# Side steps of layer 0's attention laid over a whole head, with one PSUM bank for V's sums and one for small uses

## The chip, the cores and the metric

One core of one Trainium2 chip. The metric is the device time of one execution in microseconds (us); lower is better. A core has a matrix engine (TensorE, PE in the profile; loading its weights is shown as PEld) and four others: VectorE (DVE), ScalarE (ACT), GpSimd (POOL) and SyncE (SP), which issues most transfers. Each engine carries out its own instructions in order, and waits at the first that is not ready. Data lie in SBUF (128 partitions) and matrix products are summed in PSUM, eight banks of 128 x 512 f32.

## The reference, cut to what matters

Two layers of a diffusion backbone over 1024 latent tokens and 256 context tokens, each with 1024 features. Layer 0, the one that is changed, is a multi-head latent attention with 16 heads: queries and keys have 64 columns of their own and 32 columns that are turned by a rotary table (the key's 32 are shared by all heads), values have 64.

```python
def project(t, rope):
    q_lat, kv_lat, k_pe, gate = split(t @ w_in)
    q  = (rms_norm(q_lat, g_qa) @ w_qb).reshape(b, n, 16, 64 + 32)
    kv = (rms_norm(kv_lat, g_kva) @ w_kvb).reshape(b, n, 16, 64 + 64)
    q_nope, q_pe = q[..., :64], q[..., 64:]
    k_nope, v    = kv[..., :64], kv[..., 64:]
    if rope:                      # latent tokens only
        q_pe, k_pe = apply_rope(q_pe, cos, sin), apply_rope(k_pe, cos, sin)
    return concat(q_nope, q_pe), concat(k_nope, k_pe for all heads), v, gate

o   = softmax(q   @ concat(k, k_c).T * scale) @ concat(v, v_c)   # 1024 latent queries, 1280 keys
o_c = softmax(q_c @ k_c.T * scale) @ v_c                         # 256 context queries, 256 keys
```

Layer 1 is a differential attention over the same tokens; it is not changed.

## The kernel before

Numbers are kept as pairs of f16 (a high part and the rest, H and L in the names), and a product is three matmuls: high by high, high by low, low by high. The attention of layer 0 runs from 250 to 772 us of the span, head after head (`for h in range(H0)`, the loop at the end of what is printed below). Tokens stand in three chunks of queries: b=0 and b=1 of 512 latent tokens, b=2 of 256 context tokens.

**A unit** (`units0`) is two key tiles of 128 for one chunk. `st_of` makes the scores, six matmuls of 512 columns (L834 to 836) into a pair of banks from `pair()`; ACT takes the exponential (L778) and rounds it to f16, `ph` (L779); POOL makes the rest, `pl` (L780). Two units later (`LAG`) `retire` multiplies with V: 24 matmuls (L846, L848, L849), in two halves of 12, summing over the chunk's units in one bank d. Column 64 of V is one, so the bank also holds the row's sum. Behind the last unit of a chunk `fin` divides on DVE: a reciprocal (L857) and a multiply (L858), and bank d is free after it. A head has five units for b=0, five for b=1 and one, of half the size, for b=2.

**Side steps** stand between the units on PE and make what a later chunk or head needs. `max0` finds each query's largest score: for b=0 and b=1 four wide pieces (two matmuls L758 into a pair, a reduction on DVE L760), a piece over the context keys (L764, L765, L766), then a transpose of the result on PE (L769), which DVE writes into rows of Q (L770); `st_of` of that chunk reads them. `prod_k` and `prod_q` make a head's keys and queries: `proj_pair` multiplies for two heads at once (L186 to 188), wide for 1024 latent tokens and small for 256 context tokens; `split16` makes the high part on ACT (L182) and the low part on DVE (L183); transfers on SP (`dmv`) bring the rows to the tiles KH, KL and q. Once in four heads the queries' rotary columns are made too, tile stp; their latent part goes through `rope` on DVE: a shuffle (L291), a multiply from PSUM (L292), two operations with both inputs in SBUF (L295, L296). `load_outw` (heads 13 to 15) prepares the output weights on ACT and DVE, `h1_range` (head 2) makes a scale for layer 1 in a chain of small DVE operations.

**What sets the order.** PE's order is the order of the code (`manual_schedule` with `MAN = 'P'`). The order on ACT, DVE, POOL and SP is set by a scheduler when the kernel is built, and is fixed then. `run_step` walks a list of units: the unit's `st_of`; the first half of the side steps due at it; the first half of `retire`; the other side steps; the second half of `retire`. Which steps are due is told by generators with a count for each unit. A head is two such walks, b=0, and b=1 with b=2. `set_banks(a=3, d=2)` gives three pairs to everything but V's sums, and two banks d to these.

Head numbers in this text count from 0. "Even" and "odd" heads are those numbers; keys and queries of heads 2m and 2m+1 are projected together.

Of the kernel before, what the change touches and what calls it, by code (L numbers as in the profile page):

```python
# [17 lines left out]
P = 128  # L18
# [3 lines left out]
CTX = 256  # L22
# [8 lines left out]
DQ = NOPE + ROPE  # L31
# [23 lines left out]
def hybrid_kernel(  # L55
# [690 lines left out]

    def max0(h, b):
# [14 lines left out]
        ps = pair()[:, :nt * CTX].rearrange("p (a b) -> p a b", a=nt)  # L762
# [5 lines left out]
        bk = pair()  # L768
# [116 lines left out]
    set_banks(a=3, d=2)  # L885
# [20 lines left out]
    yctx = {}  # L906
    for h in range(H0):
        last = h == H0 - 1
        even, quad = (h + 1) % 2 == 0, (h + 1) % 4 == 0
        if h == H0 - 2:  # L910
            rp.close()
            ow = ow_ctx.enter_context(spool("o0w", side="right"))
            oH = ow.tile([P, KT, D], F32R, name="oH0")
            oL = ow.tile([P, KT, D], F32R, name="oL0")
            lw = load_outw(oH, oL, lambda: w0("ows"))
        if last:
            run_step(units0(h, 0) + units0(h, 2), [(max0(h, 2), (1, 0, 1)), (max0(h, 1), (0, 1, 1, 1, 2, 1)),
                                                   (lw, (1, 0, 1))])
            octx = {t: (w0(b_), w0(a_))[::-1] for t, a_, b_ in ((8, "rsw", "rr"), (9, "cs", "cs"))}

            def load_ctx():
                yield
                yield
# [4 lines left out]
                yield  # L928

            run_step(units0(h, 1), [(load_ctx(), (1, 1, 1))])  # L930
            tv = lambda x: x.bitcast(F32R).rearrange("p (a b) -> p a b", a=KT)
            tctx = {8: (tv(w0("ows")), tv(w0("ows"))), 9: (tv(w0("rr")), tv(w0("cs")))}
            with tc.manual_schedule(engines={ENG[c] for c in MAN}):
# [7 lines left out]
                for t in (8, 9):  # L941
                    y_ = pair()
                    yctx[t] = [y_[:, :512], y_[:, 512:] if t == 8 else bank("d")]
                    for hh in range(2):
# [4 lines left out]
                        flush()  # L949
        else:  # L950
            kq = chain(prod_k(h + 1), prod_q(h + 1, 0))
            low = [[(first(lw, 3), p_)] if h == H0 - 2 else [] for p_ in ((1, 0, 1, 0, 1), (1, 0, 1, 0, 1))]
            if h == 2:
                ab1_of()
            hr = [(h1_range(pair), (0, 1, 0, 1, 1))] if h == 2 else []
            run_step(units0(h, 0), hr + [(max0(h, 1), (1, 1, 2, 1, 1)), (max0(h, 2), (0, 1, 0, 1)),
                                    (kq, (2, 2, 1 + quad, 0, 0) if even else (2,))] + low[0])
            qs = chain(prod_q(h + 1, 1), prod_q(h + 1, 2))
            run_step(units0(h, 1) + units0(h, 2), [(max0(h + 1, 0), (1, 1, 1, 2, 1)),
                                                   (qs, (1, 1 + quad, 0, 1) if even else (2,))] + low[1])  # L960
# [757 lines left out]
```

## Time and profile before

| what | value |
|---|---|
| time, median of 3 runs | 1767.51 us (1767.5 to 1769.69) |
| span of the profiled execution | 1767.7 us, 36788 instructions |
| TensorE busy (whole span) | 1660.4 us, 94% |
| VectorE, ScalarE, GpSimd busy | 1224.6 (69%), 1118.5 (63%), 821.9 us (46%) |
| layer 0's attention, 16 heads | 250.4 to 772.2 us, 521.8 us |

The page shows one execution; its span stands 0.2 us over the median. A busy engine is not one at its peak: a TensorE instruction is shown with its latency, and consecutive matmuls overlap, so the time that a matmul takes from the next is the difference between their starts. PEclk is the clock that the engine was granted, as a share of its full rate of 2.4 GHz; 0.50 is the lower level, 1.2 GHz. In a timeline the square bracket behind an operation holds how long its engine stood idle just before it and the operation that ended this.

### The profile page before, as it was taken

What the parts mean: (1) busy time and instruction counts of PE and PEld (TensorE: products, weight loads), DVE (VectorE), ACT (ScalarE), POOL (GpSimd) and SP (SyncE); (2) the same over time, 40 slices, a digit from 0 to 9 for tenths busy, and PEclk for the clock granted to TensorE, in tenths of its full rate; (3) what the DMA queues carried; (4) which work ended last, traced back from release to release, by engine and by line L of the source; (5) the groups of instructions that cost most, each with busy time, mean ns of one, the idle gap of its engine ahead of it and who ended that gap; (6) DMA issues with size and microseconds to landing.
All of it is one profiled execution on the core that took longest, in us unless ns stands there. A gap on an engine that the chain in (4) does not pass through costs nothing. (4 is left out here: it accounts for less than half of the span.)

```text
span 1767.7 us, 36788 instructions
## 1 busy us (share of the span) xinstructions
PE 1660.4 (94%) x14564; PEld 1231.8 (70%) x14564; DVE 1224.6 (69%) x2037; ACT 1118.5 (63%) x2235; POOL 821.9 (46%) x740
## 2 busy tenths in 40 slices
PE   7999989999999998899999999999999999987998
PEld 6999956556666655577867676767676767666876
DVE  7658666565565666646856778787878787878664
ACT  3551177777777778845635676767676767758542
POOL 1432147667767776845552323241424233354454
PEclk9999999999999999999999999999999999999999
DMA  8258520110111122245522222231212222142331
GB/s 308 81 152 259 166 68 21 43 44 22 42 46 25 39 57 62 65 168 196 167 96 64 80 68 80 67 81 55 60 51 63 60 58 75 32 125 66 112 108 72
DMA packets 111225, 154.84 MB, mean 88 GB/s; under 512 B 13415, under 2 KB 84679, under 8 KB 111054
## 3 DMA queue, kind: packets, MB, share of 16 engines
q1 hardware_dynamic: 102654, 144.90, 27.3%
q10 hardware_dynamic: 8400, 7.61, 1.3%
q8 instruction: 114, 1.87, 0.4%
q14 instruction: 57, 0.47, 0.1%
HBM read 98.65 MB, written 27.07 MB: 71 GB/s over the span
## 5 line engine op out<-in xcount | busy, mean ns | idle before, releaser
L780 POOL TENSOR_TENSOR pl<-p,ph 128x1024 f16<-128x1024 f32 (+1 forms) x176 | 364.3, 2076 | 148.4 <-ACT ph L779 122.6
L1371 ACT ACTIVATE p<-ps_b,mx 128x512 f32<-128x512 f32 (+1 forms) x384 | 230.2, 617 | 58.9 <-DVE mx L1367 57.4
L778 ACT ACTIVATE p<-ps_a,esc 128x1024 f32<-128x1024 f32 (+1 forms) x176 | 189.0, 1074 | 94.8 <-PE ps_a L836 88.8
L760 DVE TENSOR_REDUCE mx<-ps_a 128x1 f32<-128x1024 f32 x128 | 155.3, 1222 | 129.9 <-PE ps_a L758 129.8
L779 ACT CAST ph<-p 128x1024 f16<-128x1024 f32 (+1 forms) x176 | 177.1, 1006 | 5.5
L1365 DVE TENSOR_REDUCE mx<-ps_b 128x1 f32<-128x512 f32 x256 | 164.9, 680 | 0.7 <-PE ps_b L1349 0.7
L849 PE MATMUL ps_d<-Vh,pl 128*128 128x65 f16 x1344 | 146.0, 194 | 4.4 <-POOL pl L780 4.4
L846 PE MATMUL ps_d<-Vh,ph 128*128 128x65 f16 x1344 | 148.2, 195 | 0.0
L848 PE MATMUL ps_d<-Vl,ph 128*128 128x64 f16 x1344 | 147.0, 193 | 0.0
L846 PEld LDWEIGHTS <-ph 128*128 128x128 f16 x1344 | 123.3, 97 | 18.1 <-issue 4.9
L848 PEld LDWEIGHTS <-ph 128*128 128x128 f16 x1344 | 124.0, 98 | 12.2 <-issue 0.3
L1348 PE MATMUL ps_b<-KS,QS 128*128 128x512 f16 (+1 forms) x384 | 126.5, 347 | 5.9 <-DVE pl L183 2.9
L1349 PE MATMUL ps_b<-KS,Q 128*128 128x512 f16 (+1 forms) x384 | 129.7, 347 | 0.0
L834 PE MATMUL ps_a<-qH,KH 100*128 100x512 f16 x320 | 121.9, 381 | 7.8 <-ACT p L778 3.5
L1396 POOL TENSOR_TENSOR sm<-sm,us 128x1 f32<-128x1 f32 x64 | 18.5, 289 | 234.3 <-DVE sm L1375 221.2
L849 PEld LDWEIGHTS <-pl 128*128 128x128 f16 x1344 | 123.2, 97 | 5.8 <-POOL pl L780 5.8
L1384 PE MATMUL ps_b<-idr,p 128*128 128x128 f32 x640 | 103.8, 278 | 24.2 <-ACT p L1371 6.2
L183 DVE SCALAR_TENSOR_TENSOR pl<-ps_b,lcf,ph 128x512 f16<-128x512 f32 (+1 forms) x192 | 116.9, 653 | 11.2 <-ACT ph L182 11.2
L182 ACT ACTIVATE ph<-ps_b,lcf 128x512 f16<-128x512 f32 (+1 forms) x192 | 115.2, 647 | 13.9 <-PE ps_b L1384 13.8
L835 PE MATMUL ps_a<-qH,KL 96*128 96x512 f16 x320 | 121.8, 381 | 0.0
L836 PE MATMUL ps_a<-qL,KH 96*128 96x512 f16 x320 | 121.2, 379 | 0.0
L1384 PEld LDWEIGHTS ps_b<-idr,p 128*128 128x128 f32 x640 | 78.2, 143 | 49.0 <-ACT p L1371 11.6
(438 smaller groups left out, 5290.7 us busy)
## 6 DMA issues: line engine op xcount, KB each, us to landing
ws<-in_dw SPq DMA_DIRECT2D x28, 512.0 KB, 3.9
adw<-in_ada_w SPq DMA_DIRECT2D x24, 512.0 KB, 4.6
adaw<-in_ada_w SPq DMA_DIRECT2D x16, 512.0 KB, 7.3
g<-sg_d SPq DMA_DIRECT2D x16, 512.0 KB, 8.5
sg_d<-gg ACTq DMA_DIRECT2D x40, 128.0 KB, 3.6
o_d<-op SPq DMA_DIRECT2D x7, 640.0 KB, 3.8
xt<-in_xT SPq DMA_DIRECT2D x16, 256.0 KB, 4.4
wgs<-in_w_in SPq DMA_DIRECT2D x32, 128.0 KB, 3.1
```

The lines of the kernel that those rows point to most:

```text
L760: dve.tensor_reduce(mx[:, t, 0:1], ps, axis=AX.X, op=ALU.max)
L778: act.activation(p32[:, :n], st, AF.Exp, scale=esc0)
L779: act.copy(ph[:, :n], p32[:, :n])
L780: pool.tensor_tensor(pl[:, :n], p32[:, :n], ph[:, :n], op=ALU.subtract)
L846: pe.matmul(pv[:, t, :], ph[:, ts], Vh[:, k, h, :], start=(k == kcs[0] and t == 0), stop=False, skip_group_check=True)
L848: pe.matmul(pv[:, t, :V0], ph[:, ts], Vl[:, k, h, :], start=False, stop=False, skip_group_check=True)
L849: pe.matmul(pv[:, t, :], pl[:, ts], Vh[:, k, h, :], start=False, stop=(k == NT - 1), skip_group_check=True)
L1348: pe.matmul(out, qs[m][:, ts], ks[m][:, c0:c0 + n], start=True, stop=False)
L1349: pe.matmul(out, q1[m][:, ts], ks[m][:, c0:c0 + n], start=False, stop=True)
L1365: dve.tensor_reduce(mx[:, 2 + 2 * m + i:3 + 2 * m + i], b, axis=AX.X, op=ALU.max, negate=True)
L1371: act.activation(p[m][:, c0:c0 + n], b, AF.Exp, bias=nb, accum_out=sm[:, 2 + 3 * m + i:3 + 3 * m + i])
L1384: pe.transpose(st[:, j * P:(j + 1) * P], pc[:, (k0 + j) * P:(k0 + j + 1) * P], idn)
```

## The change

It rewrites the stage's plan and its use of PSUM; each engine has as many instructions as before.

- `set_banks(a=3, d=1, e=1)`: V's sums have one bank instead of two, and a bank e is new. `small()` hands it out, in place of a pair, to the context projections, to the context piece of b=2's row maximum, to all transposes of `max0` and to `h1_range`.
- `run_step` takes a dictionary. `sides[k, i]` lists the steps at unit k, ahead of the first (i=0) or second (i=1) half of `retire`. A head is one walk of 11 units.
- `part_k`, `part_q`, `part_p`, `load_k`, `load_q` and `top_of` take the place of the generators. In even heads the wide query projection for the pair of heads that follows now stands at unit 9, and, once in four heads (2, 6, 10), the wide rotary projection with its rope at unit 10: both stood in the odd head before. In odd heads the wide key projection stays in unit 0, the small projections in units 1 and 2.

```diff
+    def small():
+        return bank("e") if "e" in banks else pair()
     def proj_pair(cw, w2, src2, c0, n):
-        ps = pair()
+        ps = small() if n == CTX else pair()
...
+    def part_p(h, b):
+        if b == 0:
+            stH["p"] = stage("stp")
+        sH, sL = stH["p"]
+        c0, n = TOK[b]
+        cw = 1024 + (h // 4) * P
+        src = proj_pair(slice(cw, cw + P), WQ2, QS2, c0, n)
+        if b == 0:
+            sw, r = w0("rsw"), w0("rr")
+            for _ in rope(src, n, cosA, sinA, sw, r):
+                pass
+            src = r[:, :n]
+        split16(sH[:, c0:c0 + n], sL[:, c0:c0 + n], src, qsc0)
...
-        ps = pair()[:, :nt * CTX].rearrange("p (a b) -> p a b", a=nt)
+        ps = (pair if b < 2 else small)()[:, :nt * CTX].rearrange("p (a b) -> p a b", a=nt)
...
-        bk = pair()
+        bk = small()
         pe.matmul(bk[:nt, :P], ng[:, :nt], idr, start=True, stop=True)
...
+                for i in range(2):
+                    for f, *a in sides.get((k, i), ()):
+                        f(*a)
+                    if old:
+                        retire(i)
...
-    set_banks(a=3, d=2)
+    set_banks(a=3, d=1, e=1)
...
+        if h == 0:
+            put(0, 0, top_of, h, 1)
+        for k, i in ((0, 0), (1, 0), (2, 0), (3, 0), (4, 0)):
+            put(k, i, top_of, h, 1)
+        put(5, 1, top_of, h, 2)
+        put(6, 1, top_of, h, 2)
+        if n % 2:
+            put(0, 0, load_k, n)
+            put(0, 0, load_q, n, 0)
+            if n + 1 < H0:
+                put(9, 0, part_q, n + 1, 0)
+                if (n + 1) % 4 == 0:
+                    put(10, 1, part_p, n + 1, 0)
         else:
+            put(0, 1, part_k, n, 0)
+            put(1, 0, part_k, n, 1)
+            put(1, 1, part_q, n, 1)
+            put(1, 1, load_k, n)
+            put(1, 1, load_q, n, 0)
+            if n % 4 == 0:
+                put(2, 1, part_p, n, 1)
+        for k in (4, 5, 6, 7, 8):
+            put(k, 0, top_of, n, 0)
+        put(9, 1, top_of, n, 0)
+        put(6, 0, load_q, n, 1)
+        put(7, 0, load_q, n, 2)
+        put(10, 0, top_of, n, 1)
+        if h == H0 - 2:
+            for k in (0, 2, 4, 5, 7, 9):
+                put(k, 0, next, lw, None)
+        if h == 2:
+            ab1_of()
+            hr = h1_range(lambda: bank("e"))
+            for k in (1, 3, 4):
+                put(k, 0, next, hr, None)
+        run_step(units0(h, 0) + units0(h, 1) + units0(h, 2), at)
```

`n` is the next head, h + 1. In the rows below a name ends in the number of its tile; `mx` is a row maximum, `rc` and `op` are the reciprocal and the result of `fin`, `stk`, `stq` and `stp` the split keys, queries and rotary columns, `ps_a` a pair, `ps_d` and `ps_e` the single banks.

VectorE in the first units of head 3, which carries the rotary projection of the heads behind it. Before:

```order
L760 TENSOR_REDUCE mx_4315<-ps_a_4317 128x1
L857 RECIPROCAL rc_4362<-ps_d_4149 128x4
L183 SCALAR_TENSOR_TENSOR stkL_4322<-ps_a_4323,ksc_69,stkH_4321 128x1024
L183 SCALAR_TENSOR_TENSOR stkL_4322<-ps_a_4344,ksc_69,stkH_4321 128x256
L858 TENSOR_TENSOR op_4128<-ps_d_4149,rc_4362 128x4x64
L760 TENSOR_REDUCE mx_4315<-ps_a_4378 128x1
```

After, at the same place (the shuffle reads the pair that the projection at the end of head 2 filled):

```order
L291 STREAM_SHUFFLE rsw_4316<-ps_a_4303 128x1024
L292 TENSOR_TENSOR rr_4317<-ps_a_4303,cs_2545 128x1024
L295 TENSOR_TENSOR rsw_4316<-rsw_4316,cs_2549 128x1024
L813 TENSOR_REDUCE mx_4283<-ps_a_4352 128x1
L296 TENSOR_TENSOR rr_4317<-rr_4317,rsw_4316 128x1024
L183 SCALAR_TENSOR_TENSOR stkL_4369<-ps_a_4370,ksc_69,stkH_4368 128x1024
L903 RECIPROCAL rc_4391<-ps_d_4144 128x4
L813 TENSOR_REDUCE mx_4283<-ps_a_4407 128x1
L183 SCALAR_TENSOR_TENSOR stpL_4302<-rr_4317,qsc_70,stpH_4301 128x1024
L904 TENSOR_TENSOR op_4117<-ps_d_4144,rc_4391 128x4x64
L183 SCALAR_TENSOR_TENSOR stkL_4369<-ps_e_4411,ksc_69,stkH_4368 128x256
```

The rope, with its split stpL, now stands ahead of the multiply L904 that ends chunk b=1 of head 2.

VectorE at the start of head 5, an odd head without a rotary projection. Before:

```order
L760 TENSOR_REDUCE mx_5390<-ps_a_5392 128x1
L857 RECIPROCAL rc_5437<-ps_d_5224 128x4
L183 SCALAR_TENSOR_TENSOR stkL_5397<-ps_a_5398,ksc_69,stkH_5396 128x1024
L183 SCALAR_TENSOR_TENSOR stkL_5397<-ps_a_5419,ksc_69,stkH_5396 128x256
L858 TENSOR_TENSOR op_5203<-ps_d_5224,rc_5437 128x4x64
L760 TENSOR_REDUCE mx_5390<-ps_a_5453 128x1
L765 TENSOR_REDUCE mx_5457<-ps_a_5459 128x2
```

After:

```order
L903 RECIPROCAL rc_5437<-ps_d_5213 128x4
L904 TENSOR_TENSOR op_5186<-ps_d_5213,rc_5437 128x4x64
L183 SCALAR_TENSOR_TENSOR stkL_5415<-ps_a_5416,ksc_69,stkH_5414 128x1024
L813 TENSOR_REDUCE mx_5352<-ps_a_5453 128x1
L183 SCALAR_TENSOR_TENSOR stkL_5415<-ps_e_5457,ksc_69,stkH_5414 128x256
L903 RECIPROCAL rc_5493<-ps_d_5463 128x2
L183 SCALAR_TENSOR_TENSOR stqL_5296<-ps_e_5470,qsc_70,stqH_5295 128x256
```

Here the multiply stands ahead of the wide key split, and the small key split (from bank e) behind it and a row maximum; the small query projection takes bank e next.

## Rows read from the trace of the kernel before

**Rows 1.** Page, part 1: busy time, share of the span, instructions of each engine.

```profile
PE 1660.4 (94%) x14564; PEld 1231.8 (70%) x14564; DVE 1224.6 (69%) x2037; ACT 1118.5 (63%) x2235; POOL 821.9 (46%) x740
```

**Rows 2.** Windows, heads 2 to 5 and 13; columns PE, PEld, DVE, ACT, POOL, PEclk, DMA.

```profile
311.60:344.19 32.59, 29.03 (x358) 18.00 (x355) 19.84 (x38) 22.78 (x23) 22.38 (x12) 0.95 0.16 43
344.19:383.29 39.10, 36.23 (x399) 23.96 (x396) 26.42 (x34) 27.28 (x29) 23.26 (x12) 1.00 0.11 26
383.29:410.97 27.68, 26.84 (x353) 16.82 (x350) 16.37 (x23) 22.78 (x23) 22.40 (x12) 1.00 0.20 52
410.97:444.79 33.82, 32.42 (x381) 21.02 (x377) 20.01 (x27) 25.69 (x27) 22.46 (x12) 1.00 0.12 28
...
667.81:704.51 36.70, 32.92 (x381) 21.07 (x377) 25.65 (x31) 29.34 (x30) 23.26 (x11) 1.00 0.21 56
```

**Rows 3.** Timeline of PE, one unit of head 4: start, length, operation, tiles, count.

```profile
399.26 0.38 PE L834 MATMUL ps_a<-qH,KH 100*128 100x512 f16 x1
...
400.56 0.59 PE L758 MATMUL ps_a<-KH,qH 96*128 96x512 f16 x2
400.99 0.20 PE L846 MATMUL ps_d<-Vh,ph 128*128 128x65 f16 x1
...
401.71 0.38 PE L834 MATMUL ps_a<-qH,KH 100*128 100x512 f16 x1
```

**Rows 4.** Timeline of PE, head 5: wide and small query projection, and what follows each.

```profile
417.99 0.50 PE L186 MATMUL ps_a<-latH,wqH 128*128 128x512 f32 x1
...
420.85 0.20 PE L846 MATMUL ps_d<-Vh,ph 128*128 128x65 f16 x1
...
434.34 0.36 PE L186 MATMUL ps_a<-latH,wqH 128*128 128x256 f32 x1
...
435.14 0.20 PE L846 MATMUL ps_d<-Vh,ph 128*128 128x65 f16 x1
```

**Rows 5.** Timeline of ACT, POOL and DVE in the unit of rows 3.

```profile
400.82 1.11 ACT L778 ACTIVATE p<-ps_a,esc 128x1024 f32<-128x1024 f32 x1 [0.26 <-PE ps_a L836]
403.14 2.13 POOL L780 TENSOR_TENSOR pl<-p,ph 128x1024 f16<-128x1024 f32 x1 [0.32 <-ACT ph L779]
401.19 1.23 DVE L760 TENSOR_REDUCE mx<-ps_a 128x1 f32<-128x1024 f32 x1 [1.23 <-PE ps_a L758]
402.54 0.42 DVE L858 TENSOR_TENSOR op<-ps_d,rc 128x256 f32<-128x256 f32 x1
```

**Rows 6.** Groups by line and shape, 270 to 765 us: count, busy, mean ns, idle.

```profile
L183 DVE SCALAR_TENSOR_TENSOR stkL<-ps_a,ksc,stkH 128x1024 f16<-128x1024 f32 x7 | 9.0, 1284 | 0.9
L183 DVE SCALAR_TENSOR_TENSOR stkL<-ps_a,ksc,stkH 128x256 f16<-128x256 f32 x7 | 3.3, 475 | 0.0
```

**Rows 7.** Timeline of DVE and POOL around the rope in head 3.

```profile
354.28 1.29 DVE L291 STREAM_SHUFFLE rsw<-ps_a 128x1024 f32<-128x1024 f32 x1
357.85 1.23 DVE L296 TENSOR_TENSOR rr<-rr,rsw 128x1024 f32<-128x1024 f32 x1
360.32 1.84 DVE L183 SCALAR_TENSOR_TENSOR stpL<-rr,qsc,stpH 128x1024 f16<-128x1024 f32 x1
358.15 2.93 POOL L780 TENSOR_TENSOR pl<-p,ph 128x1024 f16<-128x1024 f32 x1 [3.64 <-ACT ph L779]
```

**Rows 8.** Timeline of PE: waits in head 2, and two waits in layer 1.

```profile
326.35 0.22 PE L769 MATMUL ps_a<-idr,ng 128*4 128x128 f32 x1 [1.50 <-DVE hm L301]
328.33 0.49 PE L834 MATMUL ps_a<-qH,KH 100*128 100x512 f16 x1 [1.38 <-DVE qH L770]
997.92 0.33 PE L1384 MATMUL ps_b<-idr,p 128*128 128x128 f32 x1 [2.34 <-ACT rr L1314]
1616.76 0.48 PE L1384 MATMUL ps_b<-idr,p 128*128 128x128 f32 x1 [5.57 <-DVE pl L183]
```

**Rows 9.** Windows, two stretches at the lower clock; columns as in rows 2.

```profile
328.46:331.87 3.41, 3.41 (x13) 1.33 (x12) 0.04 (x1) 0.83 (x1) 0.57 (x1) 0.50 0.00 0
1615.30:1622.10 6.80, 5.34 (x19) 2.57 (x20) 5.35 (x9) 6.37 (x18) 5.03 (x2) 0.50 0.86 302
```

More of the change, by code (lines that the diff above doesn't have):

```diff
@@ L745, in prod_q, with part_k, part_q, load_k @@
         yield
+    def part_k(h, b):
+        if b == 0:
+            stH["k"] = stage("stk")
+        sH, sL = stH["k"]
+        c0, n = TOK[b]
+        split16(sH[:, c0:c0 + n], sL[:, c0:c0 + n], proj_pair(slice(h * NOPE, h * NOPE + P), WK2, KS2, c0, n), ksc0)
+    def part_q(h, b):
+        if b == 0:
+            stH["q"] = stage("stq")
+        sH, sL = stH["q"]
+        c0, n = TOK[b]
+        split16(sH[:, c0:c0 + n], sL[:, c0:c0 + n], proj_pair(slice(h * NOPE, h * NOPE + P), WQ2, QS2, c0, n), qsc0)
+    def part_p(h, b):
+        if b == 0:
+            stH["p"] = stage("stp")
+        sH, sL = stH["p"]
+        c0, n = TOK[b]
+        cw = 1024 + (h // 4) * P
+        src = proj_pair(slice(cw, cw + P), WQ2, QS2, c0, n)
+        if b == 0:
+            sw, r = w0("rsw"), w0("rr")
[3 more added lines that the diff above has]
+        split16(sH[:, c0:c0 + n], sL[:, c0:c0 + n], src, qsc0)
+    def load_k(h):
+        i = h % 2
+        r = slice(i * NOPE, i * NOPE + NOPE)
+        for K_, j in ((KH, 0), (KL, 1)):
+            dmv(K_[i][:NOPE, :], stH["k"][j][r, :])
+    def load_q(h, b):
+        c0, n = CHUNKS[b]
+        tg = "q" if n == 512 else "qc"
+        qt[h, b] = w0(tg + "H"), w0(tg + "L")
+        r = slice((h % 2) * NOPE, (h % 2) * NOPE + NOPE)
+        rr = slice((h % 4) * ROPE, (h % 4) * ROPE + ROPE)
+        for j in range(2):
+            dmv(qt[h, b][j][:NOPE, :], stH["q"][j][r, c0:c0 + n])
+            dmv(qt[h, b][j][NOPE:DQ, :], stH["p"][j][rr, c0:c0 + n])
     def max0(h, b):
@@ L906, in hybrid_kernel, with top_of @@
     yctx = {}
+    tops = {}
+    def top_of(h, b):
+        if (h, b) not in tops:
+            tops[h, b] = max0(h, b)
+        next(tops[h, b], None)
     for h in range(H0):
         last = h == H0 - 1
-        even, quad = (h + 1) % 2 == 0, (h + 1) % 4 == 0
+        n = h + 1
         if h == H0 - 2:
@@ L915, in hybrid_kernel, with put @@
             lw = load_outw(oH, oL, lambda: w0("ows"))
+        at = {}
+        def put(k, i, *what):
+            at.setdefault((k, i), []).append(what)
         if last:
[L917 to L918 removed]
+            put(0, 0, top_of, h, 2)
+            put(2, 0, top_of, h, 2)
+            for k, i in ((0, 1), (1, 0), (2, 1), (3, 0), (4, 1)):
+                put(k, i, top_of, h, 1)
+            for k in (0, 2):
+                put(k, 1, next, lw, None)
+            run_step(units0(h, 0) + units0(h, 2), at)
             octx = {t: (w0(b_), w0(a_))[::-1] for t, a_, b_ in ((8, "rsw", "rr"), (9, "cs", "cs"))}
             def load_ctx():
[L922 to L923 removed]
                 for t in (8, 9):
@@ L942, in hybrid_kernel @@
                     y_ = pair()
-                    yctx[t] = [y_[:, :512], y_[:, 512:] if t == 8 else bank("d")]
+                    yctx[t] = [y_[:, :512], y_[:, 512:] if t == 8 else bank("e")]
                     for hh in range(2):
@@ L949, in hybrid_kernel @@
                         flush()
-        else:
[L951 to L960, printed above, removed]
+            continue
+        if h == 0:
+            put(0, 0, top_of, h, 1)
+        for k, i in ((0, 0), (1, 0), (2, 0), (3, 0), (4, 0)):
+            put(k, i, top_of, h, 1)
+        put(5, 1, top_of, h, 2)
[7 more added lines that the diff above has]
+                    put(10, 1, part_p, n + 1, 0)
+        else:
+            put(0, 1, part_k, n, 0)
[20 more added lines that the diff above has]
+        run_step(units0(h, 0) + units0(h, 1) + units0(h, 2), at)
     a0.close()
```

15 lines of the change are left out of this document (1 added, 14 removed).

## Prediction

> **What bounds the kernel now.** The list of engines comes first: TensorE is busy for 94% of the span, the next engine for 70% [rows 1]. So the end is set by TensorE's work and by the moments at which it stands. The windows by head come second, since they show where it stands. A head's fixed work can be counted from one unit: scores take 1.30 us (399.26 to 400.56), a wide piece of the row maximum 0.43, the sums with V 0.72, and the unit 2.45 in all [rows 3]. A head has ten such units, but eight wide pieces: 10 x (1.30 + 0.72) + 8 x 0.43 = 23.6. The context unit, half as large, adds 1.0; the ten matmuls of the context pieces, half as wide as those of a wide piece (0.215 each), 1.1; three transposes some 0.2. That is 26.0 us. Head 4, which has no projection of its own, took 27.68 [rows 2]: it stands for 1.7. Head 5 carries a wide query projection of 2.86 (417.99 to 420.85) and a small one of 0.80 [rows 4], and the keys' with half as many matmuls (1.43 and 0.40): 31.5 of work in 33.82, so 2.3 of standing. Head 3 has a wide and a small rotary projection besides (2.86 and 0.8): 35.1 of work in 39.10, 4.0 of standing. The pair 4/5 thus stands for 4.0, the pair of a plain even head and head 3 for 5.7. Over the whole stage that is some 50 us. The last view is the timeline of the other engines in one unit: exponential, rounding and POOL's operation (1.11, 1.2 with the gaps from 401.93 to 403.14, and 2.13, [rows 5]) follow each other at a rhythm of 2.45, and DVE has a maximum of 1.23 and little else; so between side steps nothing but TensorE is full, and every stall comes from a step that puts several DVE or ACT operations at one place.
>
> **What the change removes and adds.** The work of every engine stays as it is; only standing and clock can change.
>
> *Ordinary pairs* (0/1, 4/5, 8/9, 12/13). The wide query projection goes to unit 9 of the even head, one wide maximum stands in nearly every unit, and the small uses no longer take pairs from the scores. The scores' waits for a pair, most of the 4.0, should go. About 0.4 stays in the first unit of a head, where the context unit before it is short and POOL's pl comes late, and 0.1 for bank d. New is a wait at bank e: in units 0 and 1 of an odd head the small key and the small query projection take the one bank e with only six matmuls of V (0.2) between. From the head's start TensorE reaches the second at 1.30 + 0.43 + 0.36 + 1.43 + 0.36 + 1.30 + 0.43 + 0.40 + 0.2 = 6.2. DVE must first read bank e for the small key split, which its order puts behind the wide one and a maximum. The wide high part on ACT ends at 4.9 (scores 1.6 from 399.26 to 400.82, exponential 1.1, rounding 1.1, and the split, which I take as long as the exponential of the same shape, 1.1); then come the wide low part, 1.28, the maximum at a spacing of some 1.13, and the small split, 0.475 [rows 5, 6]: 7.8. The wait is 1.65. Queued behind it on TensorE are the rest of V's sums and the next scores, so it is on the path. Sum: 0.5 + 1.65 + 0.15 = 2.3 against 4.0, **a gain of 1.7** for each of four pairs, 6.8. The wait's bounds are 0.9 (the maximum overlapping more) and 2.2.
>
> *Heads 14 and 15.* The output weights' steps cost head 13 some 2.9 us (36.70 against 33.82, [rows 2]) and are spread as before, so I leave their cost as it is. Head 14 loses the ordinary standing and the break between its two walks, head 15 some of the first. I take **2.0** for both, between 0 and 3.
>
> *Pairs with a rotary projection* (2/3, 6/7, 10/11). Here the place decides. The wide rotary projection now ends in the last unit of the even head, and its whole chain on DVE stands ahead of the multiply that frees bank d, of which there is only one. TensorE needs that bank for the context unit's first sum, in unit 1 of the odd head. Its work from the end of the projection to there is 0.36 + 1.30 + 0.43 + 0.36 + 1.43 + 0.36 + 1.30 + 0.43 + 0.40 = 6.4. DVE's is: shuffle to last rope operation 3.45 (354.28 to 357.85, less a reciprocal of 0.12, [rows 7]), a maximum 1.13, the last rope operation 1.2, the wide key split 1.2, the reciprocal 0.15, a maximum 1.13, stpL 1.28, the multiply 0.42 [rows 5], and 0.4 for starts between engines: 10.4. The stall is 4.0 if no operation is held up. But the last rope operation and stpL read two tiles of SBUF, and rows show what such an operation and POOL's do to each other. POOL's op at 358.15 took 2.93 instead of 2.13, its first 0.9 us being those until the rope operation of 357.85 ended; stpL, begun at 360.32, took 1.84 and ended 1.08 after POOL was done at 361.08 [rows 7]. Whichever starts first, the other waits for its end. Counted from the projection's end, POOL starts unit 0's operation at 0.36 + 3.9 = 4.2 (3.9 from scores to POOL, 399.26 to 403.14), and the rope operation is ready at 4.7 to 4.8, so it waits 2.13 - 0.55 = 1.6. stpL is ready at 10.0; POOL's next start comes at 9.9, since ACT has to make stpH between the exponential and the rounding of unit 1; so stpL waits between nothing and 2. I take 0.4 for it, near the 0.56 by which stpL was longer in rows 7. The stall is then **6.0**, bounds 4.0 and 7.6. The standing of the pair becomes 6.0 + 0.5 + 0.8 (first unit and small waits at bank e, most of which passes while TensorE stands) = 7.3 against 5.7: **a loss of 1.6**.
>
> The Trainium skill (SBUF — State Buffer, "Who interferes with whom") says the same of a VectorE instruction with two SBUF inputs and a GpSimd instruction that reads SBUF, and that reductions never contend. By that rule the two maxima in the chain cost nothing more, as in the sum, and stpL would wait either nothing or for a whole operation, never 0.4: 5.6 or 7.6 in place of 6.0. The rows so far agree with it.
>
> *The clock.* Rows show what happens to the granted clock behind such a stall. In head 2, after waits of 1.50 and 1.38 close together, it was at 0.50 (1.2 GHz) for 3.41 us, all of it busy; after a wait of 5.57 it was at 0.50 for 6.80, of which TensorE was busy for 5.34; after a wait of 2.34 there was no fall [rows 8, 9]. A stall of 6.0 is nearest to that of 5.57. Work at half rate costs half its time, so a fall costs between 1.7 (3.41 / 2) and 2.7 (5.34 / 2): I take **2.2** for each of the three pairs. The Trainium skill ("TensorE: Matmul & The Clock Gate", Terms) takes the whole time at the lower clock for its penalty, not the busy part; by that it would be 3.4 each and the sum 3.6 later, which no row bears out.
>
> *Heads 2 and 3* have h1_range as well. Before, its chain of small DVE operations made waits of 1.50 and 1.38 [rows 8]. Now it stands ahead of the write of b=1's row maxima into Q, and scores wait there; the chain is the same, so I take nearly the same, 2.7, between 1.4 (one of the two) and 3.2. Before: 32.59 + 39.10 = 71.7 with 61.1 of work, so 10.6, of which 1.5 to 1.7 was clock. After: 7.3 + 2.7 = 10.0 and 2.2 of clock. **A loss of 1.6** in all; if the clock falls a second time there, 1.7 more.
>
> **Sum.** Gains 6.8 + 2.0 = 8.8. Losses 2 x (1.6 + 2.2) + 1.6 = 9.2. The profiled execution took 1767.7, the median is 0.2 lower; 1767.7 + 0.4 - 0.2 gives **1768**. What this kernel's measurement can tell from no change is about 0.2%, 3.5 us: faster means below 1764.0, slower above 1771.0. So the forecast is no change, out of two halves that cancel.
>
> **Rivals.**
> *B, the rotary chain is cheaper than I have it.* If the clock does not fall behind the three stalls, 6.6 us come back: 1761.5. The wait of 2.34 without a fall speaks for it; the stall's length, two and a half times that, against. If the operations also miss POOL's and the stall is 4.0, 6.0 more: 1755.5. It decides from two of the three falls missing. Chance 0.29, most of it near 1761.5.
> *C, slower: the clock falls behind the bank e waits too.* Each of heads 1, 5, 9 and 13 has the wait of 1.65, close behind the first unit's 0.4; in head 2 two waits of 1.4 to 1.5 were enough for a fall. Four falls at 1.7 give 6.8: 1775. It decides from two of them on. Against it stands the 2.34 without a fall. With it goes, at 1772, the rotary stall at its upper bounds (7.6, and 2.7 of clock). Chance 0.33.
> *D, the change does not do what it says.* The idle for pairs is merely renamed: scores wait for the same readers as before, and ordinary pairs gain 0 instead of 1.7, while the rotary pairs escape both losses because DVE is reached earlier. The even heads, whose standing of 1.7 has no projection in it, speak for it a little. 1767.7 less about 1: also no change. Chance 0.06.
>
> **How the numbers follow.** Forecast 0.32 and D 0.06 give 0.38 within 0.2%; B 0.29 faster; C 0.33 slower. The range takes in B's likelier value and C: 1759 to 1777. Left out are B's lower end and C with both its parts.
>
> **What would show it.** Right: in heads 3, 7 and 11 TensorE waits 5 to 7 us at the context unit's first product with V, released by DVE's multiply, and the granted clock is 0.50 right behind it; in heads 5 and 9 the small query projection waits some 1.6 for DVE's small stkL; heads 4 and 5 take 59.8 together, 6 and 7 about 70.6. Wrong: clock at 1.00 behind the rotary stall (B), at 0.50 in heads 5 and 9 (C), the multiply ahead of stpL in time, or scores that still wait for a pair in units 2 to 8 (D). The prediction falls as a whole if the stall at bank d is below 3 us, since then nothing cancels the gains.

## The result, and the profile after

The changed kernel takes 1775.04 us (median), the kernel before 1767.51: a ratio of 1.0039, 95% interval 1.0024 to 1.0053 (the two medians alone give 1.0043, inside it). It is slower, by more than the 0.2% that the measurement can tell from no change. The prediction said 1768, no change, between 1759 and 1777: the time lies inside, the likeliest case was not the one that came. The profiled execution has a span of 1773.6 against 1767.7.

The stage's heads first, from the windows of the kernel after (start and end, length, busy time and count of PE, PEld, DVE, ACT, POOL, then PEclk, DMA share, GB/s). Shown are heads 2 to 7, 11 and 13, and the three stretches at the lower clock in heads 3, 7 and 11:

```profile
313.83:348.19 34.36, 32.61 (x382) 21.54 (x378) 21.63 (x42) 24.60 (x25) 25.30 (x13) 1.00 0.16 44
348.19:387.31 39.12, 32.37 (x375) 21.03 (x371) 27.69 (x32) 25.50 (x26) 19.55 (x10) 0.91 0.10 23
387.31:416.25 28.94, 28.94 (x366) 18.75 (x363) 17.12 (x25) 24.15 (x25) 24.13 (x12) 1.00 0.19 50
416.25:447.06 30.81, 29.23 (x369) 18.94 (x366) 19.81 (x28) 24.42 (x25) 20.73 (x11) 1.00 0.13 30
447.06:479.08 32.02, 31.98 (x377) 20.99 (x374) 18.47 (x27) 24.59 (x25) 25.30 (x13) 1.00 0.18 47
479.08:517.63 38.55, 31.81 (x374) 20.90 (x371) 27.68 (x32) 25.49 (x26) 19.54 (x10) 0.91 0.10 24
609.52:649.36 39.84, 33.09 (x374) 21.28 (x371) 27.69 (x32) 25.49 (x26) 19.55 (x10) 0.87 0.13 36
678.31:715.39 37.08, 31.65 (x368) 19.68 (x365) 29.20 (x36) 31.27 (x33) 21.62 (x10) 0.95 0.40 113
358.75:365.57 6.82, 4.45 (x24) 2.94 (x25) 3.54 (x6) 0.47 (x1) 0.90 (x1) 0.50 0.27 62
488.45:495.28 6.83, 3.26 (x21) 2.51 (x22) 4.73 (x7) 0.69 (x2) 2.09 (x1) 0.50 0.25 58
618.17:628.41 10.24, 5.95 (x33) 3.61 (x34) 5.57 (x8) 2.31 (x4) 2.12 (x1) 0.50 0.35 98
```

They answer to [rows 2] and [rows 9]. Heads 4 and 5 are shorter together, 59.75 against 61.50. Heads 3, 7 and 11 have lost clock (PEclk 0.91, 0.91, 0.87; all were at 1.00 before), and TensorE stands in them; each of the three stretches begins while it still waits. Head 13 lost some clock too (0.95 against 1.00). By pairs of heads, the whole stage (from the first scores to the last product with V):

| heads | before | after | difference | predicted |
|---|---|---|---|---|
| 0 and 1 | 61.24 | 61.03 | -0.2 | -1.7 |
| 2 and 3 (rotary, h1_range) | 71.69 | 73.48 | +1.8 | +1.6 |
| 4 and 5 | 61.50 | 59.75 | -1.8 | -1.7 |
| 6 and 7 (rotary) | 66.93 | 70.57 | +3.6 | +3.8 |
| 8 and 9 | 61.59 | 59.86 | -1.7 | -1.7 |
| 10 and 11 (rotary) | 66.82 | 71.87 | +5.0 | +3.8 |
| 12 and 13 | 64.38 | 66.03 | +1.6 | -1.7 |
| 14 and 15 | 67.68 | 63.71 | -4.0 | -2.0 |
| stage | 521.83 | 526.30 | +4.5 | +0.4 |

Ahead of the stage, where the order of no engine has changed, the profiled execution after is 2.4 later (the stage begins at 252.80, before at 250.36); behind it, 1.0 earlier. Part of the 2.4 is a stretch of 3.4 at the lower clock at 27.7 us, which the profile before does not have; over the profiles of all kernels here the stage begins between 249.9 and 253.7.

What TensorE waits for over the whole stage (waits by tile and line, releaser, sum, times, longest), after:

```profile
PE ps_d L892 <- DVE op L904: 19.4, 3, 6.5
PE ps_d L895 <- POOL pl L833: 6.0, 15, 1.1
PE ps_e L186 <- DVE stkL L183: 5.5, 4, 1.4
PE ps_a L880 <- DVE qH L823: 1.7, 1, 1.7
PE ps_a L811 <- ACT p L831: 1.6, 1, 1.6
```

Three waits of 6.5 at bank d, for the multiply of `fin`, are the largest item, and did not exist before; four waits of 1.4 at bank e are new too. The rest is short. And this is why the multiply is late, in the timeline of DVE and POOL at the start of head 3, not every operation printed, with the product that waits:

```profile
348.02 1.30 DVE L291 STREAM_SHUFFLE rsw<-ps_a 128x1024 f32<-128x1024 f32 x1
351.47 1.21 DVE L813 TENSOR_REDUCE mx<-ps_a 128x1 f32<-128x1024 f32 x1
352.61 2.68 DVE L296 TENSOR_TENSOR rr<-rr,rsw 128x1024 f32<-128x1024 f32 x1
355.21 1.27 DVE L183 SCALAR_TENSOR_TENSOR stkL<-ps_a,ksc,stkH 128x1024 f16<-128x1024 f32 x1
357.60 3.13 DVE L183 SCALAR_TENSOR_TENSOR stpL<-rr,qsc,stpH 128x1024 f16<-128x1024 f32 x1
360.66 0.41 DVE L904 TENSOR_TENSOR op<-ps_d,rc 128x256 f32<-128x256 f32 x1
352.08 2.12 POOL L833 TENSOR_TENSOR pl<-p,ph 128x1024 f16<-128x1024 f32 x1 [5.22 <-issue]
357.53 2.12 POOL L833 TENSOR_TENSOR pl<-p,ph 128x1024 f16<-128x1024 f32 x1 [3.33 <-ACT ph L832]
361.12 0.23 PE L892 MATMUL ps_d<-Vh,ph 128*128 128x65 f16 x1 [6.46 <-DVE op L904]
```

The operations between 348 and 361 are those of the order that the change shows, one behind the other. Two of those with both inputs in SBUF, the last rope operation and stpL, last 2.68 and 3.13 where [rows 7] had 1.23 and 1.84. Both end 1.08 to 1.09 us behind the end of POOL's operation: 352.08 + 2.12 = 354.20 and 352.61 + 2.68 = 355.29; 357.53 + 2.12 = 359.65 and 357.60 + 3.13 = 360.73.

### The profile page after: what moved, and what is told of

Read it like the earlier page. It is cut to its first block, busy times and chain, and to the rows that moved or that the text cites. A ratio compares the mean times of both kernels' runs of the same rounds, so it can differ in the third digit from the quotient of the medians.

```text
span 1773.6 us, 36785 instructions
## 1 busy us (share of the span) xinstructions
PE 1659.1 (94%) x14564; PEld 1233.6 (70%) x14564; DVE 1236.2 (70%) x2037; ACT 1119.5 (63%) x2235; POOL 817.4 (46%) x740
## 5 line engine op out<-in xcount | busy, mean ns | idle before, releaser
L892 PE MATMUL ps_d<-Vh,ph 128*128 128x65 f16 x1344 | 149.7, 195 | 19.5 <-DVE op L904 19.4
L1479 PE MATMUL ps_b<-vh,ph 128*128 128x128 f16 x640 | 110.7, 219 | 0.0
## 6 DMA issues: line engine op xcount, KB each, us to landing
ws<-in_dw SPq DMA_DIRECT2D x28, 512.0 KB, 3.9
adw<-in_ada_w SPq DMA_DIRECT2D x24, 512.0 KB, 4.7
adaw<-in_ada_w SPq DMA_DIRECT2D x16, 512.0 KB, 7.6
g<-sg_d SPq DMA_DIRECT2D x16, 512.0 KB, 8.9
```

Of the source, the lines that this page charges most:

```text
L892: pe.matmul(pv[:, t, :], ph[:, ts], Vh[:, k, h, :], start=(k == kcs[0] and t == 0), stop=False, skip_group_check=True)
```

## The experiments

Stage lengths are from one profiled execution of each kernel, ratios from all its timed runs against the kernel before (median 1768.98 to 1771.04 beside the experiments). Where the two differ, the rest lies outside the stage, much of it clock lost in layer 1, which comes and goes (last section).

| kernel | ratio to before | 95% interval | stage |
|---|---|---|---|
| before | 1 | | 521.8 |
| after | 1.0039 | 1.0024 to 1.0053 | 526.3 |
| rope in unit 7 (e1) | 0.9975 | 0.9961 to 0.9989 | 516.3 |
| plan new, banks old (e2) | 0.9961 | 0.9947 to 0.9975 | 512.0 |
| plan old, banks new (e3) | 1.0095 | 1.0082 to 1.0108 | 532.8 |
| filler in the wait (e4) | 1.0026 | 1.0015 to 1.0037 | 522.0 |
| small query projection later (e5) | 1.0009 | 0.9998 to 1.0020 | 522.1 |
| e1 and maxima earlier (e6) | 0.9926 | 0.9910 to 0.9942 | 507.7 |
| no loads of output weights (e7) | 1.0035 | 1.0024 to 1.0045 | 530.1 |
| all moves (e8) | 0.9899 | 0.9883 to 0.9914 | 504.7 |
| all moves, one weight buffer (e9) | 0.9867 | 0.9845 to 0.9889 | 499.4 |
| low weights as zeros (e10) | 1.0023 | 1.0011 to 1.0036 | 524.5 |
| POOL only writes (e11) | 0.9975 | 0.9963 to 0.9988 | 517.2 |
| e9 with the old banks (e12) | 0.9913 | 0.9898 to 0.9928 | 505.8 |

### Is it the rope chain ahead of the multiply?

```diff
-                    put(10, 1, part_p, n + 1, 0)
+                    put(7, 1, part_p, n + 1, 0)
```

> The changed kernel with one line different: in heads 2, 6 and 10 the wide rotary projection with its rope stands in unit 7 instead of unit 10. My theory (bank d waits for a multiply that stands behind the rope chain on DVE): the wait of TensorE of 6.5 us at bank d in heads 3, 7 and 11 falls below 1 us, the granted clock stays at 1.00 there, and the time falls by 3 x (6.5 + 1.6) = 24 less some 3 for new small waits in units 7 to 10, to 1752 to 1757. Rival 1 (the chain's DVE time costs wherever it stands): at least half of it comes back as waits for pairs in units 7 to 10, 1763 to 1769. Rival 2 (the single bank d itself, whatever stands ahead of the multiply): nothing changes, 1775.

The wait at bank d is gone, and the pair 6/7 takes 66.57 instead of 70.57. That speaks against rival 2. But the median is 1764.67 (0.9975): not my 1752 to 1757, but inside rival 1's 1763 to 1769. Nor did the clock stay at 1.00 throughout: in head 3 it fell for 3.4 us, while heads 7 and 11, with the same wait of 2.6 as head 3, kept it. Pair 2/3 gained only 1.3. What TensorE waits for in this kernel from 440 to 520, and the order on DVE that makes it:

```profile
PE ps_a L880 <- DVE qH L823: 2.6, 1, 2.6
PE ps_e L186 <- DVE stkL L183: 1.4, 1, 1.4
```

```profile
473.03 2.69 DVE L296 TENSOR_TENSOR rr<-rr,rsw 128x1024 f32<-128x1024 f32 x1
475.65 0.15 DVE L819 TENSOR_REDUCE ng<-mx 128x4 fp32r<-128x8 f32 x1
476.94 1.85 DVE L183 SCALAR_TENSOR_TENSOR stpL<-rr,qsc,stpH 128x1024 f16<-128x1024 f32 x1 [1.15 <-ACT stpH L182]
478.71 1.27 DVE L183 SCALAR_TENSOR_TENSOR stqL<-ps_a,qsc,stqH 128x1024 f16<-128x1024 f32 x1
480.02 0.74 DVE L823 SCALAR_TENSOR_TENSOR qH<-ps_e,sh,selt 4x512 f16<-4x512 f32 x1
```

The same chain now stands ahead of another short operation that TensorE needs: L823, which writes the next head's row maxima into Q. Not the chain's time as such came back, but its place ahead of L823. If so, the maxima need only be earlier (the rope stays in unit 7):

```diff
+        if n % 2:
+            put(3, 1, top_of, n, 0)
+            for k in (4, 5, 6, 7):
+                put(k, 0, top_of, n, 0)
+            put(8, 1, top_of, n, 0)
+        else:
+            for k in (4, 5, 6, 7, 8):
+                put(k, 0, top_of, n, 0)
+            put(9, 1, top_of, n, 0)
```

> The kernel with the rope in unit 7, and besides in even heads the next head's row maxima one unit earlier, so that their write into Q (L823) stands ahead of stpL and stqL on DVE. Theory (the 2.7 us that came back there are a wait for that write behind two splits): the scores of heads 3, 7 and 11 start without a wait, the pair 6/7 takes 63.0 to 64.0 (70.6 in the changed kernel, 66.6 with the rope in unit 7 alone), the granted clock stays at 1.00 in it, and the whole is some 9 shorter than with the rope alone: ratio 0.991 to 0.993. Rival (the chain's time on DVE must be paid somewhere): the pair stays above 65.5, ratio 0.996 or more.

The ratio is 0.9926 and the clock of heads 6, 7, 10 and 11 stays at 1.00. The pair 6/7 takes 65.48: better than 66.57, not the 63 to 64 that I expected, and at the rival's limit. The wait for L823 (9.4 in four waits with the rope alone, 300 to 660 us) is 1.2 in one, that of h1_range; what took its place are three waits of 1.0 for ACT's exponential at the first scores of heads 3, 7 and 11. So the place was most of it, and about 1 us per pair is not a matter of place on DVE. Another 1.4 per pair is the wait at bank e: heads 3, 7 and 11 now have it too, where before it passed while TensorE stood at bank d.

### The size of the chain: what POOL adds

```diff
-        pool.tensor_tensor(pl[:, :n], p32[:, :n], ph[:, :n], op=ALU.subtract)
+        if fill:
+            pool.memset(pl[:, :n], 0.0)
+        else:
+            pool.tensor_tensor(pl[:, :n], p32[:, :n], ph[:, :n], op=ALU.subtract)
...
+            return (kc, *softmax_parts(st, 2 * n, h in (3, 7, 11) and b == 0 and kc < 4))
```

> The changed kernel, in which POOL, in units 0 and 1 of heads 3, 7 and 11, writes zeros to pl instead of reading p and ph (the low part of the probabilities of these units is left out). DVE's and TensorE's orders stay as they are. Theory (the last rope operation and stpL are held until POOL's reading operation ends): they take 1.2 and 1.3 instead of 2.7 and 3.1, and TensorE's wait at bank d falls from 6.5 to 3.0 to 3.5; the whole is 10 to 14 shorter with the clock, ratio 0.996 to 0.998. Rival 1 (any operation of POOL holds them): they still last until POOL's operation ends, the wait stays above 5. Rival 2 (the length of the two on DVE has another reason, such as their operands): 2.7, 3.1 and 6.5 stay, ratio 1.004.

Waits of TensorE in this kernel from 300 to 660, and DVE in head 3:

```profile
PE ps_d L895 <- DVE op L907: 9.5, 3, 3.2
```

```profile
353.44 1.21 DVE L296 TENSOR_TENSOR rr<-rr,rsw 128x1024 f32<-128x1024 f32 x1
357.00 1.28 DVE L183 SCALAR_TENSOR_TENSOR stpL<-rr,qsc,stpH 128x1024 f16<-128x1024 f32 x1
358.20 0.42 DVE L907 TENSOR_TENSOR op<-ps_d,rc 128x256 f32<-128x256 f32 x1
```

1.21, 1.28 and 3.2, as the theory has it: of a wait of 6.5, 3.3 is POOL's hold and 3.2 the chain itself. Rival 2 falls. Rival 1 does not quite: POOL's writes ran at once, at 347.6 and 349.3, ahead of both operations, so this run shows what they take while POOL stands, not what a write on POOL at the same moment would do.

### What the clock cost

Twenty matmuls were put into the wait, in the small key projection's own bank:

```diff
+        for _ in range(fill):
+            pe.matmul(ps[:, :512], w2[0][0][:, cw], src2[0][0][:, :512], start=True, stop=True)
```

> The changed kernel with 20 matmuls of 512 columns (some 4.6 us) added ahead of the small key projection of heads 4, 8 and 12, in its own bank, whose results are overwritten: TensorE works through most of its wait for bank d instead of standing. Work is added and no wait is shortened. Theory (the clock falls because TensorE stands): the granted clock stays at 1.00 behind it in heads 3, 7 and 11, and the time falls by what slow matmuls cost in the profile of the changed kernel (excess over the usual spacing of 1.9, 1.3 and 2.4 us), 4 to 5 in all: 1770 to 1771. Rival (the falls do not come from this standing): the falls remain and the time is 1775 or later.

Work was added, and heads 3, 7 and 11 became 0.4, 1.3 and 1.2 shorter, 2.9 together; the stage 4.3. TensorE still waits at bank d behind the filler, 1.96 each time. Windows of this kernel behind those three waits:

```profile
358.80:362.20 3.40, 3.37 (x17) 2.31 (x17) 0.84 (x4) 0.47 (x1) 0.00 (x0) 0.51 0.48 111
484.00:492.00 8.00, 6.00 (x41) 4.34 (x40) 6.18 (x9) 2.24 (x5) 2.14 (x1) 1.00 0.21 48
618.20:621.60 3.40, 3.40 (x22) 2.46 (x23) 1.11 (x4) 0.47 (x1) 0.00 (x0) 0.51 0.63 129
```

In head 7 the clock stayed at 1.00, in heads 3 and 11 it fell for 3.4 us instead of 6.8 and 10.2. So the falls do come with the standing, and became shorter with it, but were not all gone; a wait of 2 was left, which may be why. The expectation held in its sign, and its 4 to 5 us were too much (ratio 1.0026, 1.0013 less than the changed kernel, some 2 us, with intervals that overlap).

### Bank e

```diff
-            put(1, 1, part_q, n, 1)
...
+            put(2, 0, part_q, n, 1)
             if n % 4 == 0:
-                put(2, 1, part_p, n, 1)
+                put(3, 1, part_p, n, 1)
```

> The changed kernel with the small query projection of the odd heads moved from unit 1 to the start of unit 2 (and the small rotary one from unit 2 to unit 3). Theory (it waits for bank e because the small key split is late on DVE): the wait of 1.55 us in heads 1, 5, 9 and 13 goes, each of these heads is 1.5 shorter (head 5 from 30.8 to 29.3), heads 3, 7 and 11 stay, and the whole is 6 us shorter: ratio to the kernel before about 1.0005. Rival (DVE is loaded there and the wait moves on to the next step that needs DVE): head 5 stays above 30.2 and the whole is shorter by 2 at most, ratio 1.003.

Heads 1, 5 and 9 fell to 29.2 each (30.9, 30.8, 30.9 before this edit), no wait of these projections for bank e is left, and the ratio is 1.0009: the theory, within its interval. Head 13 did not follow. It takes 37.98 instead of 37.09, with new waits of 2.4 for `ng` and 2.5 at bank d, so the stage is 4.2 shorter and not 6.

### Plan and banks apart

The new plan with `set_banks(a=3, d=2)`, `small()` falling back on pairs:

> The changed kernel's plan with the old banks: two banks d, no bank e, and small uses take pairs again. My theory: the context unit's first product finds a free bank d, so the wait of 6.5 goes from there, but the small key and query projections then wait for pairs that DVE is late to read, so 2 to 4 us of it come back in heads 3, 7 and 11; the waits of 1.55 at bank e in heads 1, 5, 9, 13 become 0 to 0.6. Time 1757 to 1765. Rival (the plan, not the banks, costs the time): 1772 to 1776, with waits for pairs as long as the one for bank d was.

And the old plan with one bank d, bank e and `small()`:

> The old plan with the new banks: one bank d, one bank e, small() as in the change. My theory: in the odd heads the multiply of chunk b=1 stands behind both key splits on DVE, so the context unit's first product waits 1 to 2 us for bank d in seven heads; small uses no longer wait for pairs, which gives back about 1 per pair of heads. Time 1767 to 1776, most likely 1771. Rival (the banks are what gains in the ordinary pairs): 1764 or less. Second rival (the banks alone make the loss): 1775 or more with waits for bank d over 3 us.

This is the clearest result, and not what I had. Stage lengths: 521.8 with old plan and old banks, 512.0 with the new plan alone, 532.8 with the new banks alone, 526.3 with both. The plan gains 10, the banks cost 11 in the old plan and 14 in the new. For the plan alone the theory held (0.9961, 1761.8, in its range), for the banks alone it missed: I expected 1771, it is 1785. Waits in the two kernels around heads 6 and 7, plan alone (472.6 to 507.6) and banks alone (440 to 520):

```profile
PE ps_a L811 <- DVE stkL L183: 0.9, 1, 0.9
PE ps_a L186 <- ACT p L831: 0.8, 1, 0.8
PE ps_a L186 <- DVE stkL L183: 0.6, 1, 0.6
```

```profile
PE ps_d L850 <- DVE op L862: 2.0, 1, 2.0
PE ps_e L186 <- DVE stpL L183: 1.7, 1, 1.7
```

With the old banks the waits are for pairs, several and short. With the new ones a wait for bank d is 2.0 in the old plan too, because the rope stands ahead of a multiply there as well, and bank e adds one of 1.7 behind stpL. Both waits stand once in each of heads 3, 7 and 11, and nowhere else; my theory had bank d's in seven heads. The loss lies in the rotary pairs alone: they take 78.20, 70.67 and 69.11 where the kernel before takes 71.69, 66.93 and 66.82, while the other pairs are up to 0.7 shorter. Clock is part of it: in head 2 it fell for 6.8 (3.4 before), in head 3 twice and in head 7 once for 3.4 each, in head 11 not at all. My second rival's time came (1775 or more), but not its waits of over 3 at bank d.

Nor is it the banks as such. With the waits moved away (next part) the same two arrangements stand the other way:

> The last version (all moves, output weights through one buffer) with the old banks: two banks d, no bank e, small uses take pairs. Theory (one bank d costs only where something long stands ahead of the multiply on DVE, and the moves have taken that away): the stage stays within 3 us of that version's 499.4, ratio to the kernel before 0.985 to 0.989. Rival 1 (the new banks cost by themselves, as the old plan with them did, by 11 us in the stage): 8 to 14 us less in the stage, ratio 0.978 to 0.982. Rival 2 (bank e is a gain now that its wait is gone): 4 us or more slower, ratio 0.989 to 0.991.

505.8 with the old banks, 499.4 with the new: rival 2, though its ratio came out at 0.9913. One bank d and a bank e are worth 6 us here and cost 14 in the changed kernel. What differs between the two comparisons are all the moves together. That it is what stands on DVE ahead of the operations that free the banks fits the waits (19.4 for the multiply in the changed kernel, 1.7 in this one), but no run turned the sign by that alone.

### Head 13, and all moves together

Heads 12 and 13 should have gained 1.7 and lost 1.6. In head 13 ACT stands 1.7 us for a load of the output weights, so the first suspicion was ACT's queue:

> The changed kernel with six of the eight loads of the output weights of layer 0 left out: ACT and DVE do the same operations on the first two blocks again (which part of the computation is left out: the other six blocks of these weights). Theory (ACT stands in its queue for these loads, and exponentials and scores behind it): ACT waits no longer for a transfer in heads 13 and 14, head 13 falls from 37.1 to 31 to 34 and its clock stays at 1.00; the whole is 3 to 6 shorter, ratio 1.0005 to 1.002. Rival (the operations themselves are too dense on ACT and DVE): head 13 stays above 36, ratio 1.0035 or more.

It fell. Without six of the eight loads head 13 takes 40.09, more than the 37.08 with them. Most of the difference is clock, which was low for 10.2 us instead of 3.4; half of TensorE's busy time there, 8.54 and 3.41, makes an estimate of 2.6 of the 3.0. What this kernel's DVE does in head 13:

```profile
692.07 2.65 DVE L922 SCALAR_TENSOR_TENSOR oL<-ows,usc,oH 128x1024 fp32r<-128x1024 f32 x1
694.65 0.15 DVE L819 TENSOR_REDUCE ng<-mx 128x4 fp32r<-128x8 f32 x1
694.72 3.08 DVE L922 SCALAR_TENSOR_TENSOR oL<-ows,usc,oH 128x1024 fp32r<-128x1024 f32 x1
697.83 0.74 DVE L823 SCALAR_TENSOR_TENSOR qH<-ps_e,sh,selt 4x512 f16<-4x512 f32 x1
```

Two operations with both inputs in SBUF, 2.65 and 3.08 long, stand ahead of `ng` and L823, which TensorE waits for (2.6 and 1.3): the picture of the rope again. So the second theory was that these alone are the loss:

```diff
-            dve.scalar_tensor_tensor(oL[:, k, :], ws, usc0, fv(oH[:, k, :]), op0=ALU.mult, op1=ALU.subtract)
+            dve.memset(fv(oL[:, k, :]), 0.0)
```

> The changed kernel with the eight low parts of the output weights left out: DVE writes zeros there instead, with no input to read (the low part of these weights is what is left out); loads and ACT's part stay. Theory (DVE's two-input operations, held up by POOL, are head 13's loss): head 13 falls from 37.1 to 30.8 to 32.5, its clock stays at 1.00, the whole is 5 to 6 shorter, ratio 1.0005 to 1.0015. Rival (ACT's steps or its waits for loads are the loss): head 13 stays above 35, ratio 1.003 or more.

Head 13 takes 36.40: this theory missed as well. The trace of the changed kernel had spoken against it: there none of the eight lasts over 1.60 us, so POOL held them up little, and the long ones belong to the kernel without the loads. The clock of head 13 stayed at 1.00, but TensorE now waits for ACT's exponentials too (1.2 and 0.8, from 679 to 716 us); ACT's eight steps stand as close as before. Neither the loads nor DVE's part is the loss by itself; how it is shared between ACT's and DVE's steps stays open.

The moves together, with h1_range in head 4 and head 0's second piece later:

```diff
-            put(0, 0, top_of, h, 1)
+            put(0, 1, top_of, h, 1)
...
-        if h == 2:
+        if h == 4:
             ab1_of()
             hr = h1_range(lambda: bank("e"))
-            for k in (1, 3, 4):
+            for k in (5, 6, 8):
```

> All moves together: rope in unit 7, row maxima of even heads one unit earlier, the small query projection in unit 2, head 0's second piece in the other half of unit 0, and the h1_range steps in units 5, 6 and 8 of head 4 instead of 1, 3 and 4 of head 2. If each of the waits is a separate one, as I hold: ordinary pairs 58.2 to 58.6, rotary pairs 61.5 to 63, the stage 490 to 500 us (521.8 before, 526.3 changed), the whole 1738 to 1748 where the kernel before takes 1767.5: ratio 0.983 to 0.989. If they share DVE's time (rival): 0.992 or more.

0.9899, just outside, and the stage is 4.7 longer than the range. The plain ordinary pair is where I had it (8/9 58.45); 0/1 and 4/5, which holds h1_range now, take 59.6. The rotary pairs are a little longer (6/7 63.96), and head 13 takes 41.61, with two falls of the clock. Then the weights through one buffer:

```diff
-            lw = load_outw(oH, oL, lambda: w0("ows"))
+            lw = load_outw(oH, oL, lambda: w0("rsw"))
```

> All moves together as before, and the output weights go through one buffer instead of two, so that the next load, and the operations on ACT and DVE behind it, can't follow sooner than one step is done; the order then spreads DVE's eight low parts (two inputs in SBUF) over heads 13 to 15. Theory (head 13 loses its time because these operations stand close together ahead of the row maxima's write into Q, and are held up by POOL): head 13 falls from 41.6 to 31 to 34, the stage from 504.7 to about 495, ratio to the kernel before 0.983 to 0.986. Rival (loads in ACT's queue are the cost: one buffer makes ACT wait more): head 13 and 14 together stay above 68, ratio 0.989 or more.

Head 13 takes 33.55 (31.08 for head 14), the stage 499.4, where about 495 was expected, and the clock does not fall in it. Of DVE's eight low parts four stand in head 13 and four in head 14, as in the kernel before; in the version ahead of it, as in the changed kernel, all eight stood in head 13. At 1745.76 us and 0.9867 (0.9845 to 0.9889) this version beats both kernels; the ratio is a little above what I expected.

## Why the prediction was right or wrong

- **What bounds the kernel**: right. TensorE's work is the same in all these kernels but the one with the filler; the stage's length followed its waits and its clock throughout. The 70% read as the next engine's is PEld, TensorE's own weight load; the next engine is VectorE with 69% [rows 1].
- **Rotary pairs, the wait at bank d**: right, in mechanism and nearly in size. 6.0 was said, 6.5 measured in each of the three heads (the timeline above, against [rows 7]). Of the terms, POOL's hold of the rope operation was said to be 1.6 and was 1.5. That of stpL was said to be 0.4 "near the 0.56 by which stpL was longer in rows 7"; it was 1.9. The step that failed is the choice of a middle value for something that has none: stpL was ready 0.1 us behind POOL's start and waited for the whole operation. The sentence on the Trainium skill (SBUF — State Buffer, "Who interferes with whom") had said just this, nothing or a whole operation, and this case agrees with it: 3.13 and 2.68, each ending 1.1 behind POOL. The chain without POOL was said to make a stall of 4.0 and made 3.2, which made up for half of it; that 6.5 is so near to 6.0 is luck in part.
- **Rotary pairs, the clock**: right on average, wrong in spread. The prediction's own estimate, half of TensorE's busy time at the lower clock, makes 2.2, 1.6 and 3.0 of the three stretches, where 2.2 was said for each. 70.6 was said for the pair 6/7, 70.57 measured, and that is luck in part: 0.5 more of stall stood against 0.6 less of clock. In 10/11 the lower clock lasted 10.2 us instead of 6.8, 1.3 more. In head 2 the scores' wait behind h1_range was said to be 2.7 and was 1.7.
- **Ordinary pairs**: 4/5 and 8/9 gained 1.75 and 1.74 where 1.7 was said, with the wait at bank e of 1.4 (said 1.65, where its own terms, 7.8 less 6.2, give 1.6), which one edit removed. The 0.15 beside it in that sum has no row. But the reason given was half wrong. That "the small uses no longer take pairs" was not what gained: with pairs for the small uses, the same plan has 59.12 for 4/5, 0.6 less than with bank e. The plan gained all of it. Bank e paid only once its wait was moved away: 4/5 takes 58.09 with the small query projection later.
- **Pair 0/1**: wrong, -0.2 for -1.7. I carried the sum of the ordinary pair over; head 0, which gets no row maxima from a head before it, makes one wide piece more and has waits of its own, 0.8 for ACT's exponential and 0.5 for a maximum, which head 4 does not have.
- **Heads 12 to 15**: the step "spread as before, so I leave their cost as it is" failed. The new plan lets the scheduler put the steps of the output weights wholly into head 13 (eight of DVE's eight low parts, four before): 3.3 worse than said for 12/13, 2.0 better for 14/15, 1.4 worse together.
- **Sum**: the stage came out 4.1 later than said: +3.3 (12/13), -2.0 (14/15), +1.5 (0/1), +1.3 (10/11), +0.2 (2/3), -0.2 in the others. Another 2.4 of the profiled execution lies ahead of the stage.
- **Rivals**: slower was given 0.33 by a fall of the clock behind the waits at bank e. That rival's mechanism did not come: heads 1, 5 and 9 kept 1.00, and the one fall in head 13 begins 17 us behind its wait at bank e, next to a wait of 1.6 for ACT's exponential. It was slower for the terms above. The range's upper end rested on that rival, so that 1775 lies inside is luck in part. The 1772 that the rival gives for the rotary stalls at their upper bounds is too low: three times 1.6 and three times 0.5 make 1774. B (no fall, or no hold by POOL) did not come either; D neither.

## What to carry to other kernels

A PSUM bank is as good as the promptness of the operation that frees it: before taking a second bank away, list what stands ahead of that operation on its engine at each hand-over, with the length each has while other engines run. When a long chain is moved off one short operation that the bound engine waits for, look for the next such operation behind it; here it was first the multiply that frees bank d, then the write of the row maxima. And where a change has two parts, run each alone: plan and banks had opposite signs, and the sign of the banks turned once the moves together had taken the chains out of their way.

## What the runs showed of the hardware

Where the granted clock falls is partly chance. Layer 1 has three waits for the same ACT operation, some 95 us apart, of 1.5 to 2.3 us in the profiles before, after and with the rope in unit 7. Two of them, in the kernel after and in that with the rope in unit 7, and the windows 1.0 to 1.1 us behind:

```profile
1004.86 0.33 PE L1471 MATMUL ps_b<-idr,p 128*128 128x128 f32 x1 [1.92 <-ACT rr L1401]
```

```profile
1006.00:1009.40 3.40, 3.40 (x34) 3.11 (x32) 0.51 (x3) 3.40 (x13) 1.05 (x2) 1.00 0.17 43
```

```profile
993.79 0.33 PE L1471 MATMUL ps_b<-idr,p 128*128 128x128 f32 x1 [1.93 <-ACT rr L1401]
```

```profile
994.83:998.25 3.42, 3.42 (x19) 2.68 (x17) 0.53 (x3) 3.42 (x13) 1.15 (x2) 0.50 0.17 44
```

The same wait, 1.92 and 1.93, and the clock is at its full rate behind the one and at the lower level for 3.4 us behind the other. Between 970 and 1300 us, the fourteen profiled kernels, whose code there is the same, have between none and four such stretches (before two, after none). One wait of layer 1, for a DVE operation, is 1.97 or 1.98 in all fourteen: such a stretch begins within 1.4 us behind it in seven of them, and in the other seven none does. With some 1.7 us each (half of 3.4) this moves one execution by several us, which is why single profiles are compared by stage here. So the prediction's "after a wait of 2.34 there was no fall" was one draw, not a rule; and the filler run shows the same for three waits of 1.96, of which two were followed by a fall. The waits of 6.5 were never without one: in the four profiles that have all three of them unchanged (after, e5, e7 and e10), each of the twelve has a stretch of 6.8 or 10.2 at the lower clock.
